# A one-layer hybrid decoder trunk: stick-breaking scans that read PSUM, full-width low products, one engine for four copies, and the second gate's row built in another stage

## The chip, the cores and the metric

One core of a Trainium2 chip runs the kernel. The metric is the device time of one execution in microseconds (us), as the median of several runs. Five engines work side by side, each through its own instructions in a fixed order: TensorE (PE, matrix products and transposes), VectorE (DVE), ScalarE (ACT), GpSimd (POOL) and SyncE (SP), which issues most of the DMAs here. They wait for one another through semaphores.

## The reference

One layer, 1024 tokens, width 1024, float32. What is computed:

```python
mod = silu(c) @ ada_w + ada_b
sh1, sc1, g1, sh2, sc2, g2 = split(mod, 6)
h = rms_norm(x, norm1_g) * (1 + sc1) + sh1
x = x + g1 * (concat(GLA(h), Retention(h), StickBreaking(h)) @ w_out)
h = rms_norm(x, norm2_g) * (1 + sc2) + sh2
x = x + g2 * swiglu(h, ffn_wg, ffn_wu, ffn_wd)
out = rms_norm(x, final_g)
```

GLA is gated linear attention (4 heads, key width 32), Retention has 4 heads of width 64, and stick-breaking attention has 8 heads of width 64:

```python
z = q @ k.T / 8
attn[t, s] = sigmoid(z[t, s]) * prod(1 - sigmoid(z[t, j]) for s < j < t)    # s < t
```

## The kernel before

The program has stages. A prologue normalises the tokens and makes the first projections (to about 98 us of the profiled execution). Then comes the **mixer**, about 100 to 700 us: the rest of the input projection, the three mixers, and the output projection in two halves. The **up stage**, about 700 to 1155 us, makes the two SwiGLU products, and the **down stage** the last product and the output. A float32 product is made of three single-pass matmuls: each operand is split into a high part and a low part (`split`, `split_to`), and `mm3` (L68 to L70) multiplies high by high, low by high and high by low.

In the mixer the dense projections are a generator that yields after every few microseconds of matmuls. At each yield the streams `ada`, `gla`, `ret` and `sb` are advanced to where a hand-written pace puts them (`Stream`, L786 to L789). What comes out is then ordered by the tile scheduler, which lays the instructions of each engine in its own order; so a change in one place moves instructions in others.

**Stick-breaking** (`sb_stream`). For each of 8 heads and 8 blocks of 128 queries, `weights` makes scores `z` in PSUM, in groups of up to 512 columns: 96 groups in all, through two PSUM banks (pool `pz`, two buffers). ACT turns each `z` into two sigmoids in SBUF: `u` = sigmoid(-z) (L410) and `At` = sigmoid(z) (L411). A DVE scan from right to left turns `u` into a running product in place (L418), and POOL multiplies `At` by it (L58, tile `s_a`). PE transposes the weights (L435, one bank, `tr`), ACT and DVE split them into `s_th` and `s_tl`, and `products` multiplies them with the values, whose high and low halves stand side by side as 64 and 64 columns of one stationary tile `V` (L454 to L457, one bank, `av`). The high weights meet both halves. The low weights meet the high half only, so that those matmuls write 64 of the 128 partitions. ACT and DVE then add the two halves into `s_o` (L461, L462).

**Gated linear attention** (`gla_stream`). Four blocks of 256 tokens, seven levels each. At each level four strips of `q` are copied into a block tile `g_qb`, two by DVE and two by ACT (L607), PE multiplies (L612), and DVE masks and scales.

**Modulation rows.** `ada_vec` (L281) makes one 1024-wide slice of `mod`: DVE clears `grow`, and for each of eight 512 KB loads of `ada_w` ACT scales the tile by silu(c) and POOL adds it into `grow`. `ada_row` (L291) sums over partitions with two PE products with a tile of ones. `ada_stream` runs slices 3, 4, 5 and 2 in the mixer. Slice 5 is the second gate g2: it goes to DRAM (`d_g2`, L310) and is loaded again ahead of the down stage (L1077). Slice 2, the first gate, is folded into the weights of the output projection.

**Up stage.** For each of 11 column groups and two weights, seven products of 512 columns run through eight PSUM banks in rotation (`bank`, `nps`). POOL and DVE make sums of the weights (`operands`, tile `st`); at its start, `t1` to `t4` are sums and differences of the normalised tokens (tiles `x`, `hb`, `to`).

Of the kernel before, what the change touches and what calls it, by code (L numbers as in the profile page):

```python
# [7 lines left out]
F32 = mybir.dt.float32  # L8
# [3 lines left out]
ALU = mybir.AluOpType  # L12
# [27 lines left out]
def tile_hybrid(ctx, tc, x, c, ada_w, ada_b, norm1_g, norm2_g, w_in, gla_wa2, gla_ba,  # L40
# [235 lines left out]


    grow = const.tile([P, D], F32, name="grow")
    d_g2 = dram.tile([P, D], F32, name="d_g2")

    def ada_vec(i):  # L281
        DVE.memset(grow, 0.0)
        nc.scalar.dma_start(grow[0:1, :], ada_b[:, i * 1024:(i + 1) * 1024])
        for k in range(8):
            raw = gp.tile([P, 1024], F32, name="a_raw", bufs=2)
            nc.sync.dma_start(raw, aw[k * P:(k + 1) * P, i * 1024:(i + 1) * 1024])
            ACT.activation(raw, raw, AF.Copy, scale=sil[:, k:k + 1])  # L287
            tt(POOL, grow, grow, raw, ALU.add)
            yield

    def ada_row(i):  # L291
        yield from ada_vec(i)
        for b in range(2):
            ps = dn.tile([P, NH], F32, name="dn")
            PE.matmul(ps, ones, grow[:, b * NH:(b + 1) * NH], start=True, stop=True)
            ACT.copy(grow[:, b * NH:(b + 1) * NH], ps)
        yield
# [7 lines left out]
    def ada_stream():  # L305
        yield from ada_cols(3, B2)
        yield from ada_cols(4, modc[:, 0:8])
        DVE.scalar_tensor_tensor(out=A2, in0=modc[:, 0:8], scalar=1.0, in1=cols[:, 16:24], op0=ALU.add, op1=ALU.mult)
        yield from ada_row(5)
        nc.scalar.dma_start(d_g2, grow)  # L310
        yield from ada_row(2)


# [58 lines left out]
    def sb_stream(pool, pz, ptr, pav):  # L372
# [22 lines left out]
        def weights(ops_, i):  # L395
            Q, K1, K2, _ = ops_
            W = (i + 1) * P
            At = pool.tile([P, NH * (1 + i // 4)], F32, name=f"s_a{i // 4}", bufs=4)
            carry = None
            for c0 in ((512, 0) if W > 512 else (0,)):  # L400
                w = min(W - c0, 512)
                z = pz.tile([P, NH], F32, name="z")
                q = Q[:, i * P:(i + 1) * P]
                diag = c0 + w == W
                PE.matmul(z[:, :w], q, K1[:, c0:c0 + w], start=True, stop=False)
                PE.matmul(z[:, :w], q, K2[:, c0:c0 + w], start=False, stop=not diag)
                if diag:
                    PE.matmul(z[:, w - P:w], identb, maskb, start=False, stop=True)
                u = pool.tile([P, 520], F32, name="s_u", bufs=2)
                ACT.activation(u[:, :w], z[:, :w], AF.Sigmoid, scale=-0.125)  # L410
                ACT.activation(At[:, c0:c0 + w], z[:, :w], AF.Sigmoid, scale=0.125)  # L411
                if carry is None:
                    POOL.memset(u[:, w:w + 1], 1.0)
                else:
                    DVE.tensor_copy(u[:, w:w + 1], carry)
                carry = u[:, 0:1]
                ur = u[:, 0:w][:, ::-1]
                DVE.tensor_tensor_scan(ur, ur, zero.broadcast_to([P, w]), u[:, w:w + 1], op0=ALU.mult, op1=ALU.add)  # L418
                tt(POOL, At[:, c0:c0 + w], At[:, c0:c0 + w], u[:, 1:w + 1], ALU.mult)
            return At  # L420

# [25 lines left out]
        def products(hd, i, g, V, th, tl):  # L447
            if g == i // 2:
                acc_ps[0] = pav.tile([P, 256], F32, name="av")
            ps = acc_ps[0]  # L450
            for sj in (1, 0):
                s_ = 2 * g + sj
                if s_ == i:
                    PE.matmul(ps, V[:, s_, :, :], th[:, sj, :], start=True, stop=False)  # L454
                PE.matmul(ps[0:64], V[:, s_, 0, :], tl[:, sj, :], start=False, stop=False)
                if s_ != i:
                    PE.matmul(ps, V[:, s_, :, :], th[:, sj, :], start=False, stop=(s_ == 0))  # L457
            if g == 0:
                done_sb[0] += 1
                o2 = pool.tile([64, 256], F32, name="s_o2", bufs=2)  # L460
                ACT.copy(o2, ps[64:128])  # L461
                tt(DVE, o2, o2, ps[0:64], ALU.add)  # L462
                nc.sync.dma_start(d_mix[4 + hd // 2][i // 4][64 * (hd % 2):64 * (hd % 2) + 64, (i % 4 - 1) * P:(i % 4 + 1) * P], o2)
# [78 lines left out]
    def gla_stream(pool, pg):  # L542
# [33 lines left out]
        for bi in range(4):  # L576
# [23 lines left out]
            for l in range(NLEV):  # L600
                m = 1 << l
                nb = P // m
                kv = k32.rearrange("p (b e m) -> p b e m", e=2, m=m)
                qv = q32.rearrange("p (b e m) -> p b e m", e=2, m=m)
                for h in range(4):
                    r = slice(32 * h, 32 * h + 32)
                    (ACT.copy if h % 2 else DVE.tensor_copy)(  # L607
                        QB[l % 2][r, h, :].rearrange("p (b m) -> p b m", m=m), qv[r, :, 1, :])
                yield
                ps = pg.tile([P, 8, 64], F32, name="g")  # L610
                for c_ in range(2):
                    PE.matmul(ps[:, 4 * c_:4 * c_ + 4, :], k32[:, c_ * P:(c_ + 1) * P],  # L612
                              QB[l % 2][:, :, c_ * 64:(c_ + 1) * 64], start=(c_ == 0), stop=(c_ == 1))
                so = Sm.rearrange("p h (b e m) -> p h b e m", e=2, m=m)[:, :, :, 1, :]
                mk = gm[:, l * 64:(l + 1) * 64].rearrange("p (b m) -> p b m", m=m).unsqueeze(1).broadcast_to([P, 8, 64 // m, m])
                DVE.copy_predicated(so, mk, ps.rearrange("p h (b m) -> p h b m", m=m))
                Tv = T.rearrange("p (b e) -> p b e", e=2)
                tt(DVE, qv[:, :, 1, :], qv[:, :, 1, :], Tv[:, :, 0:1].broadcast_to([P, nb, m]), ALU.mult)
                tt(DVE, kv[:, :, 0, :], kv[:, :, 0, :], Tv[:, :, 1:2].broadcast_to([P, nb, m]), ALU.mult)
                if l == 2 and fin:  # L620
                    fin()
                    fin = None
                T2 = pool.tile([P, P], F32, name="g_t", bufs=2)[:, :nb]
                tt(DVE, T2, Tv[:, :, 0], Tv[:, :, 1], ALU.mult)
                T = T2
# [160 lines left out]
    gla = Stream(gla_stream(gp, pgp), [65, 0], [225, 76])  # L786
    ret = Stream(ret_stream(pgp), [216, 0], [248, 41])
    sb = Stream(sb_stream(sbp, pz, ptr, pav), [0, 0], [123.5, 60], [265, 152])
    ada = Stream(ada_stream(), [20, 0], [185, 36])  # L789
    active = [ada, sb]  # L790

    def in_units():
# [230 lines left out]
    for j in range(4):  # L1023
# [6 lines left out]
        for lst, r in ((t3, r12), (t2, r22), (t4, r21)):  # L1030
            op = halves(tp.tile([P, D], F32R, name="to"))
            lst.append(split_to((op[:, 0], op[:, 1]), r))

    for i in range(NF // 2):
        gate = None
        for w in range(2):
            c0, c1, c2, c3 = early[w] if i == 0 else first_two(i, w)
            silu(w, c0)
            mid = ("s2", t2), ("s3", t3), ("a22", t4), ("s1", t1)
            if i == w == 0:  # L1040
                p6, p7, p4, p5 = products(i, w, *mid)
            else:
                p6, p7, p4, p5 = None, None, None, None
            p6 = p6 if p6 is not None else products(i, w, mid[0])
            tt(DVE, c1, c1, p6, ALU.add)
            p7 = p7 if p7 is not None else products(i, w, mid[1])
            tt(DVE, c2, c1, p7, ALU.add)
            p4 = p4 if p4 is not None else products(i, w, mid[2])
            tt(DVE, c3, c2, p4, ALU.add)
            silu(w, c3)  # L1050
            p5 = p5 if p5 is not None else products(i, w, mid[3])
            tt(DVE, c2, c2, p5, ALU.add)
            tt(DVE, c1, c1, p5, ALU.add)
            silu(w, c2)
            tt(DVE, c1, c1, products(i, w, ("s4", b22)), ALU.add)
            silu(w, c1)
            if w == 0:
                gate = c0, c1, c3, c2
            else:


                a11, a21, a12, a22 = gate
                s3, s1, s4, s2 = c0, c1, c3, c2
                for g_, u_ in zip((a11, a21, a22, a12), (s3, s1, s2, s4)):
                    tt(POOL, g_, g_, u_, ALU.mult)
                tt(POOL, s3, a11, a21, ALU.subtract)
                tt(POOL, s2, a22, s3, ALU.subtract)
                tt(DVE, s1, a21, a22, ALU.add)
                tt(DVE, s4, a12, s2, ALU.subtract)
                for n, a in (("a11", a11), ("a12", a12), ("a22", a22), ("s3", s3), ("s2", s2), ("s1", s1), ("s4", s4)):  # L1070
                    nc.scalar.dma_start(d_g[i][n], a)
# [2 lines left out]

    nc.sync.dma_start(grow, d_g2)  # L1077
    xe.close()
    kp = ctx.enter_context(tc.tile_pool(name="kp", bufs=8))
    ct = [halves(kp.tile([P, D], F32, name="ct")) for t in range(8)]  # L1080
# [202 lines left out]
```

## Time and profile before

| | us |
|---|---|
| median of 3 runs | 1379.72 (1377.66 to 1384.37) |
| the profiled execution, its own time | 1378.98 |
| its span, first to last instruction | 1377.1 |
| PE busy | 1271.5 (92%) |
| DVE busy | 994.4 (72%) |
| POOL busy | 750.1 (54%) |
| ACT busy | 626.3 (45%) |

The span lies 1.9 us under the time of the same execution, and that time 0.7 us under the median. Busy shares are averages over stages with different limits: PE is busy nearly all the time in the up stage and has gaps in the mixer, so the mixer's waits are read by themselves. The granted clock of PE is at its upper level nearly everywhere and at the lower one in short pieces.

### The profile page before, as it was taken

The page shows a single profiled execution, that of the slowest core. Times are in us where ns is not written, and L with a number is a line of the kernel's source. Part 1 is how long each engine was busy: PE and PEld are TensorE (multiplying, and loading weights), DVE is VectorE, ACT ScalarE, POOL GpSimd, SP SyncE. Part 2 cuts the span into 40 slices and gives each one's busy share as a digit, 9 for nine tenths or more (in the row PEclk, how much of TensorE's full clock was granted, in tenths as well). Part 3 has the DMA queues.
Part 4 walks back from the last instruction along what each step waited for, and adds up shares of the span by engine and source line. Part 5 has one row for each costly group of instructions (what it writes and reads, how often), then busy time and mean ns, then how long its engine had stood idle before and what let it go on. Part 6 is the DMA issues. An engine that isn't in the chain of part 4 may idle for free.

```text
span 1377.1 us, 20202 instructions
## 1 busy us (share of the span) xinstructions
PE 1271.5 (92%) x7076; PEld 1096.4 (80%) x7076; DVE 994.4 (72%) x1376; ACT 626.3 (45%) x1198; POOL 750.1 (54%) x732
## 2 busy tenths in 40 slices
PE   2899998989979998998998999999999999999996
PEld 1678897779868888898986888888888887888874
DVE  5604666898798968888579756655666558989996
ACT  3445675565555645444365333323333324544344
POOL 4737445355473435674157555555455534647893
PEclk9999999999999999999998999999999999999998
DMA  9537536263443237413432333332332346755333
GB/s 308 186 101 224 161 108 196 89 177 104 136 141 89 62 101 237 148 50 101 150 121 86 107 115 114 101 110 89 107 107 93 107 143 221 246 165 187 116 122 123
DMA packets 141026, 187.62 MB, mean 136 GB/s; under 512 B 19230, under 2 KB 94167, under 8 KB 140923
## 3 DMA queue, kind: packets, MB, share of 16 engines
q1 hardware_dynamic: 112416, 148.90, 35.5%
q10 hardware_dynamic: 28508, 37.43, 7.9%
q8 instruction: 56, 0.92, 0.3%
q14 instruction: 46, 0.38, 0.1%
HBM read 138.77 MB, written 47.51 MB: 135 GB/s over the span
## 4 chain that ended last, share of the span: by engine, by line
PE 54%; DVE 22%; DMA 9%; issue 7%; POOL 4%; ACT 4%; SPq 0%; DVEq 0%; ACTq 0%; POOLq 0%
PE m L69 7%; PE m L70 7%; PE m L68 7%; PE dn L69 6%; PE dn L68 6%; PE dn L70 6%; DVE s_u L418 4%; PE tr L69 3%; PE tr L70 3%; PE tr L68 3%; DVE acc L210 3%; DMA a_raw<-in_ada_w_dram 2%; DVE to L58 2%; POOL grow L58 1%; DVE hl L58 1%
## 5 line engine op out<-in xcount | busy, mean ns | idle before, releaser
L68 PE MATMUL dn<-whi,hh 128*128 128x256 f32 (+1 forms) x768 | 224.0, 292 | 0.4 <-ACT st L337 0.3
L70 PE MATMUL dn<-whi,hl 128*128 128x256 f32 (+1 forms) x768 | 222.7, 290 | 0.0
L69 PE MATMUL dn<-wlo,hh 128*128 128x256 f32 (+1 forms) x768 | 221.4, 288 | 0.2 <-DVE wlo L58 0.2
L58 POOL TENSOR_TENSOR s_a<-s_a,s_u 128x128 f32<-128x128 f32 (+3 forms) x96 | 98.8, 1033 | 130.2 <-DVE s_u L418 66.5
L68 PEld LDWEIGHTS dn<-whi,hh 128*128 128x128 f32 x768 | 148.3, 193 | 2.8 <-ACT st L337 0.6
L69 PEld LDWEIGHTS dn<-wlo,hh 128*128 128x128 f32 x768 | 148.3, 193 | 1.8 <-DVE wlo L58 0.4
L70 PEld LDWEIGHTS dn<-whi,hl 128*128 128x128 f32 x768 | 148.2, 193 | 0.8
L418 DVE TENSOR_TENSOR_SCAN s_u<-s_u,zero 128x128 f32<-128x128 f32 (+3 forms) x96 | 119.1, 1248 | 33.2 <-ACT s_u L410 20.3
L58 POOL TENSOR_TENSOR st<-raw 128x512 f32<-128x512 f32 x44 | 68.8, 1563 | 89.0 <-DMA raw<-in_ffn_wg_dram 65.3
L58 POOL TENSOR_TENSOR grow<-grow,a_raw 128x1024 f32<-128x1024 f32 x32 | 79.5, 2484 | 47.0 <-ACT a_raw L287 25.3
L58 POOL TENSOR_TENSOR x<-x,x 128x512 f32<-128x512 f32 x55 | 78.7, 1432 | 41.5 <-DVE x L58 39.6
L64 ACT CAST s_th<-tr 128x512 fp32r<-128x512 f32 (+2 forms) x112 | 48.7, 435 | 63.0 <-DVE s_tl L58 36.2
L58 DVE TENSOR_TENSOR s_tl<-tr,s_th 128x512 fp32r<-128x512 f32 (+2 forms) x112 | 54.9, 490 | 30.0 <-ACT s_th L64 29.7
L58 DVE TENSOR_TENSOR x<-x,m 128x512 f32<-128x512 f32 x79 | 52.8, 682 | 22.1 <-PE m L70 21.1
L58 DVE TENSOR_TENSOR wlo<-raw,whi 128x1024 fp32r<-128x1024 f32 (+2 forms) x32 | 42.1, 1319 | 33.5 <-ACT whi L64 33.3
L58 DVE TENSOR_TENSOR wlo<-st,wlo 128x512 fp32r<-128x512 f32 x44 | 47.9, 1088 | 24.0 <-ACT wlo L914 23.3
L58 DVE TENSOR_TENSOR to<-whi,to 128x512 fp32r<-128x512 f32 x53 | 55.8, 1054 | 11.7 <-ACT to L914 11.7
L58 POOL TENSOR_TENSOR st<-raw,st 128x512 f32<-128x512 f32 x22 | 28.9, 1315 | 63.9 <-DVE whi L58 37.8
L914 ACT CAST to<-whi 128x512 fp32r<-128x512 f32 x53 | 32.9, 620 | 62.7 <-PE m L70 24.6
L914 ACT CAST wlo<-raw 128x512 fp32r<-128x512 f32 x33 | 20.5, 621 | 85.9 <-POOL x L58 64.6
L914 ACT CAST wlo<-st 128x512 fp32r<-128x512 f32 x44 | 27.4, 622 | 70.7 <-DVE x L58 29.4
L410 ACT ACTIVATE s_u<-z 128x128 f32<-128x128 f32 (+3 forms) x96 | 46.5, 491 | 28.0 <-POOL s_a L58 12.5
(374 smaller groups left out, 4079.8 us busy)
## 6 DMA issues: line engine op xcount, KB each, us to landing
a_raw<-in_ada_w_dram SPq DMA_DIRECT2D x32, 512.0 KB, 4.9
raw<-in_ffn_wg_dram SPq DMA_DIRECT2D x22, 512.0 KB, 3.9
raw<-in_ffn_wu_dram SPq DMA_DIRECT2D x22, 512.0 KB, 3.9
hb<-in_ffn_wd_dram SPq DMA_DIRECT2D x44, 256.0 KB, 3.6
d_g_s<-x ACTq DMA_DIRECT2D x44, 256.0 KB, 2.0
whi<-d_g_s SPq DMA_DIRECT2D x44, 256.0 KB, 3.1
raw<-in_w_in_dram SPq DMA_DIRECT2D x20, 512.0 KB, 3.9
d_g_a<-x ACTq DMA_DIRECT2D x33, 256.0 KB, 2.9
```

What stands on the lines that cost most here:

```text
L58: eng.tensor_tensor(out=o, in0=a, in1=b, op=op)
L64: ACT.copy(hi, src)
L68: PE.matmul(o, sh, mh, start=start, stop=False)
L69: PE.matmul(o, sh, ml, start=False, stop=False)
L70: PE.matmul(o, sl, mh, start=False, stop=stop)
L210: DVE.scalar_tensor_tensor(out=acc[:, cs_[s]], in0=ab[s, h][:, k, :], scalar=sil[:, 4 * h + k:4 * h + k + 1], in1=acc[:, cs_[s]], op0=ALU. ...
L410: ACT.activation(u[:, :w], z[:, :w], AF.Sigmoid, scale=-0.125)
L418: DVE.tensor_tensor_scan(ur, ur, zero.broadcast_to([P, w]), u[:, w:w + 1], op0=ALU.mult, op1=ALU.add)
L914: ACT.copy(op[0], src)
```

## The change

Four edits. The second sigmoid is written back into the PSUM bank of `z`, and the scan reads it there and writes `u` in SBUF; the sigmoid for `At` comes first. The low weights multiply both value halves. All four copies of a GLA level are on ACT. The row for g2 is made in the loop of the up stage, from its second column group on, through the buffers `hb`, and its two sums take banks of the up stage's rotation; the trip through DRAM is gone. The pace of `ada` ends at step 27 in place of 36.

```diff
-    d_g2 = dram.tile([P, D], F32, name="d_g2")
-
-    def ada_vec(i):
+    def ada_vec(i, raw_of=None):
         DVE.memset(grow, 0.0)
         nc.scalar.dma_start(grow[0:1, :], ada_b[:, i * 1024:(i + 1) * 1024])
         for k in range(8):
-            raw = gp.tile([P, 1024], F32, name="a_raw", bufs=2)
+            raw = raw_of() if raw_of else gp.tile([P, 1024], F32, name="a_raw", bufs=2)
             nc.sync.dma_start(raw, aw[k * P:(k + 1) * P, i * 1024:(i + 1) * 1024])
...
-    def ada_row(i):
-        yield from ada_vec(i)
+    def ada_row(i, raw_of=None, bank_of=None):
+        yield from ada_vec(i, raw_of)
         for b in range(2):
-            ps = dn.tile([P, NH], F32, name="dn")
+            ps = bank_of() if bank_of else dn.tile([P, NH], F32, name="dn")
...
-        yield from ada_row(5)
-        nc.scalar.dma_start(d_g2, grow)
         yield from ada_row(2)
...
                 u = pool.tile([P, 520], F32, name="s_u", bufs=2)
-                ACT.activation(u[:, :w], z[:, :w], AF.Sigmoid, scale=-0.125)
                 ACT.activation(At[:, c0:c0 + w], z[:, :w], AF.Sigmoid, scale=0.125)
+                ACT.activation(z[:, :w], z[:, :w], AF.Sigmoid, scale=-0.125)
...
-                DVE.tensor_tensor_scan(ur, ur, zero.broadcast_to([P, w]), u[:, w:w + 1], op0=ALU.mult, op1=ALU.add)
+                DVE.tensor_tensor_scan(ur, z[:, 0:w][:, ::-1], zero.broadcast_to([P, w]), u[:, w:w + 1], op0=ALU.mult, op1=ALU.add)
...
-                PE.matmul(ps[0:64], V[:, s_, 0, :], tl[:, sj, :], start=False, stop=False)
+                PE.matmul(ps, V[:, s_, :, :], tl[:, sj, :], start=False, stop=False)
...
                 for h in range(4):
                     r = slice(32 * h, 32 * h + 32)
-                    (ACT.copy if h % 2 else DVE.tensor_copy)(
-                        QB[l % 2][r, h, :].rearrange("p (b m) -> p b m", m=m), qv[r, :, 1, :])
+                    ACT.copy(QB[l % 2][r, h, :].rearrange("p (b m) -> p b m", m=m), qv[r, :, 1, :])
...
-    ada = Stream(ada_stream(), [20, 0], [185, 36])
+    ada = Stream(ada_stream(), [20, 0], [185, 27])
...
+    def next_bank():
+        nps[0] += 1
+        return bank(nps[0] - 1)
+
+    g2 = ada_row(5, lambda: tp.tile([P, D], F32, name="hb", bufs=4), next_bank)
     for i in range(NF // 2):
         gate = None
+        if i:
+            next(g2, None)
...
-    nc.sync.dma_start(grow, d_g2)
+    for _ in g2:
+        pass
     xe.close()
```

The scheduler's order moves with it. On DVE, in one level of gated linear attention (`g_s` is the masked product, `g_k` and `g_q` the scaled strips, `s_tl` and `s_u` belong to stick-breaking), it was:

```order
L616 COPY_PREDICATED g_s<-gm,g 128x256x2
L58 TENSOR_TENSOR g_k<-g_k,g_t 128x64x2
L607 COPY g_qb_2484<-g_q 32x128 x2
L58 TENSOR_TENSOR g_t<-g_t 128x32
L58 TENSOR_TENSOR g_q<-g_q,g_t 128x16x8
```

and is now:

```order
L612 COPY_PREDICATED g_s<-gm,g 128x128x4
L58 TENSOR_TENSOR g_k<-g_k,g_t 128x32x4
L58 TENSOR_TENSOR g_t<-g_t 128x16
L58 TENSOR_TENSOR g_q<-g_q,g_t 128x8x16
L58 TENSOR_TENSOR s_tl<-tr,s_th 128x512
```

The pair of copies is out of DVE's order in every level. On ACT, at the start of the fifth head of stick-breaking, the sigmoids of two groups and what surrounds them were:

```order
L410 ACTIVATE s_u<-z 128x128
L411 ACTIVATE s_a_3713<-z 128x128
L296 COPY grow<-dn 128x512
L410 ACTIVATE s_u<-z 128x256
L411 ACTIVATE s_a_3762<-z 128x256
```

and are now:

```order
L407 ACTIVATE s_a_3688<-z 128x128
L408 ACTIVATE z<-z 128x128
L407 ACTIVATE s_a_3731<-z 128x256
L408 ACTIVATE z<-z 128x256
L64 CAST s_th<-tr 128x512
```

The sigmoid that the scan needs stands second, and it writes `z`. On POOL, at the start of the up stage (`hb<-x,hb`, `x<-x,hb` and `hb<-hb,x` make the token sums, `st` the weight sums), it was:

```order
L58 TENSOR_TENSOR x_8282<-x_8282,x_8353 128x512
L58 TENSOR_TENSOR hb<-hb,x_8248 128x512
L58 TENSOR_TENSOR hb<-hb 128x512
L58 TENSOR_TENSOR x_8265<-x_8265,hb 128x512
L58 TENSOR_TENSOR hb<-hb 128x512
L58 TENSOR_TENSOR hb<-hb,x_8265 128x512
L58 TENSOR_TENSOR hb<-hb 128x512
L58 TENSOR_TENSOR st<-raw 128x512
L58 TENSOR_TENSOR st<-st,raw 128x512
```

and is now:

```order
L58 TENSOR_TENSOR hb<-hb,x_8206 128x512
L58 TENSOR_TENSOR x_8223<-x_8223,hb 128x512
L58 TENSOR_TENSOR grow<-grow,hb 128x1024
L58 TENSOR_TENSOR hb<-hb,x_8223 128x512
L58 TENSOR_TENSOR grow<-grow,hb 128x1024 x2
L58 TENSOR_TENSOR st<-raw 128x512
L58 TENSOR_TENSOR grow<-grow,hb 128x1024
L58 TENSOR_TENSOR st<-st,raw 128x512
L58 TENSOR_TENSOR st<-raw 128x512
L58 TENSOR_TENSOR grow<-grow,hb 128x1024
```

Though the loop asks for one step of the row per column group, the scheduler draws all eight additions to the start of the stage, among the last token sums and the first weight sums. `hb<-hb` were differences of the down weights, loaded ahead; they stand later now.

## Rows read from the trace of the kernel before

**Rows 1.** Busy time by stretch: window, length, PE, PEld, DVE, ACT, POOL, PEclk, DMA, GB/s.

```profile
100.00:700.00 600.00, 552.69 (x3927) 508.20 (x3925) 457.82 (x719) 326.36 (x677) 302.52 (x397) 0.98 0.45 133
...
780.00:1150.00 370.00, 370.00 (x1634) 306.38 (x1633) 222.32 (x295) 119.98 (x202) 188.02 (x133) 1.00 0.36 114
```

**Rows 2.** Waits of PE, 100 to 700 us: total us, times, longest us.

```profile
PE av L454 <- DVE s_o L58: 14.1, 6, 4.3
PE tr L435 <- DVE s_tl L58: 11.2, 11, 2.5
PE g L612 <- DVE g_k L58: 4.8, 4, 2.4
...
PE z L405 <- ACT s_a L411: 1.9, 4, 0.6
```

**Rows 3.** Groups of DVE by shape, 100 to 700 us: busy us, mean ns, idle before.

```profile
L418 DVE TENSOR_TENSOR_SCAN s_u<-s_u,zero 128x512 f32<-128x512 f32 x48 | 76.7, 1599 | 7.4 <-ACT s_u L410 5.6
...
L58 DVE TENSOR_TENSOR s_tl<-tr,s_th 128x512 fp32r<-128x512 f32 x48 | 32.7, 680 | 20.5 <-ACT s_th L64 20.4
...
L607 DVE COPY g_qb<-g_q 32x128 f32<-32x128 f32 x56 | 19.7, 351 | 0.5
...
L58 DVE TENSOR_TENSOR wlo<-raw,wlo 128x512 fp32r<-128x512 f32 x1 | 0.7, 678 | 0.0
```

**Rows 4.** The scan's line: ns min/median/max of all shapes.

```profile
L418 DVE TENSOR_TENSOR_SCAN s_u<-s_u,zero x96: 468/1272/3120, 118.0 to 612.0; 128x512 f32<-128x512 f32 x48, 128x128 f32<-128x128 f32 x16, 128x256 f32<-128x256 f32 x16, 128x384 f32<-128x384 f32 x16
```

**Rows 5.** Timeline of DVE, 280 to 292.4 us: start, us, instruction.

```profile
280.72 2.98 DVE L418 TENSOR_TENSOR_SCAN s_u<-s_u,zero 128x512 f32<-128x512 f32 x1 [0.40 <-ACT s_u L410]
...
285.01 2.54 DVE L607 COPY g_qb<-g_q 32x128 f32<-32x128 f32 x2
...
288.71 1.28 DVE L418 TENSOR_TENSOR_SCAN s_u<-s_u,zero 128x512 f32<-128x512 f32 x1
```

**Rows 6.** Timeline of POOL, the same stretch.

```profile
280.21 2.41 POOL L58 TENSOR_TENSOR grow<-grow,a_raw 128x1024 f32<-128x1024 f32 x1 [3.36 <-ACT a_raw L287]
...
285.06 2.41 POOL L58 TENSOR_TENSOR grow<-grow,a_raw 128x1024 f32<-128x1024 f32 x1
```

**Rows 7.** Timeline of PE, the same stretch; in brackets the idle time before.

```profile
285.24 1.10 PE L612 MATMUL g<-g_qb,g_k 128*128 128x256 f32 x4 [1.99 <-ACT s_o L461]
...
292.19 0.55 PE L454 MATMUL av<-s_th,s_v 128*128 128x256 f32 x1 [3.10 <-DVE s_o L58]
```

**Rows 8.** Busy time by stretch, behind those gaps.

```profile
286.00:300.00 14.00, 10.90 (x62) 10.14 (x61) 12.56 (x22) 5.89 (x12) 5.78 (x4) 0.76 0.58 152
```

**Rows 9.** Groups of ACT by shape, 100 to 700 us.

```profile
L287 ACT ACTIVATE a_raw<-a_raw,sil 128x1024 f32<-128x1024 f32 x32 | 36.9, 1154 | 35.1 <-DMA a_raw<-in_ada_w_dram 33.5 <-POOL s_a L58 1.6
...
L607 ACT COPY g_qb<-g_q 32x128 f32<-32x128 f32 x56 | 16.7, 298 | 21.5 <-DVE g_q L58 6.6 <-PE g L612 4.7 <-POOL g_qb L571 3.2
```

**Rows 10.** Groups of POOL by shape, 100 to 700 us.

```profile
L58 POOL TENSOR_TENSOR grow<-grow,a_raw 128x1024 f32<-128x1024 f32 x32 | 79.5, 2484 | 47.0 <-ACT a_raw L287 25.3 <-DMA grow<-in_ada_b_dram 18.6 <-DVE s_tl L58 2.7
```

**Rows 11.** Timeline of PE, 300 to 325 us: the two kinds of value products.

```profile
307.42 0.28 PE L457 MATMUL av<-s_th,s_v 128*128 128x256 f32 x1
307.53 0.28 PE L455 MATMUL av<-s_tl,s_v 128*64 128x256 f32 x1
307.65 0.28 PE L457 MATMUL av<-s_th,s_v 128*128 128x256 f32 x1
```

**Rows 12.** Busy time by stretch at the start of the up stage.

```profile
720.00:740.00 20.00, 14.03 (x50) 9.82 (x50) 20.00 (x17) 14.48 (x24) 18.14 (x11) 0.83 0.20 62
740.00:760.00 20.00, 18.31 (x73) 14.76 (x74) 16.91 (x21) 6.34 (x11) 13.27 (x10) 0.91 0.35 110
760.00:780.00 20.00, 20.00 (x89) 16.54 (x89) 15.50 (x22) 6.61 (x12) 13.74 (x10) 1.00 0.36 116
```

**Rows 13.** A group of POOL, 710 to 790 us.

```profile
L58 POOL TENSOR_TENSOR hb<-hb 128x512 f32<-128x512 f32 x4 | 6.2, 1548 | 4.5 <-DMA hb<-in_ffn_wd_dram 4.5
```

**Rows 14.** A group of PE, 100 to 700 us.

```profile
L295 PE MATMUL dn<-grow,ones 128*128 128x512 f32 x8 | 4.3, 616 | 0.0
```

## The prediction

> **What bounds the kernel now.** I read first the busy time by stretch. In the up stage PE is busy 370.00 of 370.00 us at full clock: nothing that is taken from another engine there can shorten it. In the mixer, 100 to 700 us, PE is busy 552.69 of 600, so it stands idle 47.3 us, and a mean granted clock of 0.98 says that about 2% more, 12 us, is lost in pieces at the lower level [rows 1]. Those 59 us are what the first three edits can win. Second, the waits of PE in that stretch: the two longest sums end at DVE, at the add that empties the bank of the value products (14.1 us in 6 waits) and at the low split that frees the transpose bank (11.2 in 11), and the third at a DVE scaling (4.8 in 4). These are 30.1 of the 47.3 us [rows 2]. DVE itself is busy 457.82 of 600 us [rows 1]. So PE waits because DVE comes late to short jobs that PE needs, each behind other work in DVE's fixed order.
>
> Third, what that other work is. A 512-column scan takes 1599 ns in the mean [rows 3], yet 1.28 us at 288.71 us [rows 5]; the longest scan of all takes 3120 [rows 4]. The long ones run beside a POOL operation: the scan of 2.98 us that starts at 280.72 lies over a 2.41 us addition of POOL that starts at 280.21, and the pair of copies that takes 2.54 us at 285.01 lies over the next one at 285.06 [rows 5, 6]. The low split `s_tl`, which reads one operand in PSUM, has a mean of 680 ns over 48, the same as the 678 of an undisturbed split that reads two from SBUF [rows 3]. So with one operand in PSUM the stretching is gone, and there is no surcharge for reading PSUM.
>
> Fourth, one piece of the timeline shows how that reaches PE: it stood idle 1.99 us before 285.24 and 3.10 us before 292.19 [rows 7]. The first gap lies behind the stretched scan, the second behind the stretched copies, with DVE working nearly without a break in between. [...]
>
> **The change part by part.** *Scans.* With the stretching gone, 48 x (1.60 - 1.28) = 15.3 us leave DVE. Of the 48 shorter scans I count nothing in the sum.
> [...]
>
> *Copies.* 56 copies, 19.7 us, leave DVE [rows 3]. ACT does their like in 298 ns, 16.7 us for 56, and takes them on [rows 9]. ACT is busy 326.36 of 600 us [rows 1], and the g2 row takes 8 x 1.154 = 9.2 us away from it there [rows 9], so it ends about 7 us fuller: room enough. A level's four strips now follow one another, 4 x 0.30 instead of 2 x 0.30 us, on 28 levels; I cost that at nothing, since PE has dense products to do in the meantime. If that cover failed it would be at most 28 x 0.6 = 16.8 us.
>
> *The g2 row.* Eight POOL additions of 2484 ns, 19.9 us [rows 10], leave the mixer, a quarter of the 32 that stretch two-operand work on DVE. What DVE's other instructions gain from that I leave out.
>
> Together DVE loses 15.3 + 19.7 = 35 us of 458. How much of that is PE's? In the piece shown, the scan shrinks by 2.98 - 1.28 = 1.70 of the gap of 1.99, and the pair of copies goes entirely, 2.54 of the gap of 3.10 [rows 5, 7]: 4.2 of 5.1 us, 83%. A gap whose run of DVE work holds neither piece gives 0. Between those ends I take the middle, 40%: 12.0 of the 30.1 us of waits, and 40% of the 12 us lost to the clock, 4.8, since the low pieces stand behind such gaps. **Gain 16.8 us**, with 0 and 35 as its ends (83% of 42.1).
>
> *The bank of `z`.* It is given back when the scan has ended, and no longer when ACT has read it. PE waits today for ACT at 4 of 96 groups, 1.9 us in all [rows 2]. Each such wait grows by the scan, 1.28 to 1.60 us: 4 x 1.28 = 5.1 us if DVE starts at once. Behind a wait for `z` on PE stand dense products, which wait too. Against it, the scheduler knows the new wait and may leave more work between two groups. Ends 0 and, as the rival below, 31; I take 2, nearest to the few waits that exist.
>
> *Low products.* 160 matmuls now fill 128 columns. In the row of products, the 64-column one starts at 307.53 and the next at 307.65, 0.12 us; the 128-column one at 307.42 is followed after 0.11 [rows 11]. So the moving 256 columns set the pace, and the edit costs nothing on PE. Were every one to pay the difference of these slots in the other direction, 160 x 0.01 = 1.6 us, it would be a gain; I take 0.
>
> *The row in the up stage.* Two products of 616 ns go into a stage where PE never rests: 1.2 us [rows 1, 14]. The eight additions, 19.9 us, are drawn to the start of the stage, where four differences of the down weights, 6.2 us, had been [rows 13]: 13.7 us more of POOL. From 720 to 780 us POOL is busy 18.14 + 13.27 + 13.74 = 45.2 of 60, so they fit into the 14.8 us that are free, but only just; PE is idle 6.0 us of the first 20 there, and DVE is busy all of them [rows 12]. Most token sums stand ahead of the additions in POOL's order, and the first weight sums between them. Cost between 0 and 13.7; I take 2, near the low end, since PE is full from 760 on. Eight loads of 512 KB and 9.2 us of ACT lie under the stage's DMA share of 0.36 and ACT's 120 of 370 us [rows 1].
>
> Sum: -16.8 + 2 + 1.2 + 2 = **-11.6 us**. The profiled execution took 1378.98, so 1367.4; it lies 0.7 us under the median of the runs, so against that I say **1368 us**.
>
> **The rivals.** *More than forecast.* If the other gaps are like the piece shown, 83% of 42.1 us come back: 35 - 5 = 30 us, 1350. For it: the three DVE jobs of rows 2 are short, and 35 us go from the queue ahead of them. Against: many gaps stand behind masks, splits and rotations that stay.
>
> *Nothing arrives.* DVE gets lighter, but PE waits for the next engine: ACT, with 7 us more, stands just ahead of DVE in every split, and the sigmoid that the scan needs now comes second. Or the scan from PSUM stretches all the same, as it still reads the zero operand in SBUF. Then costs and gain cancel: 1376 to 1384.
>
> *Slower: the two banks of `z` become the pace.* A bank is now held through both sigmoids, DVE's queue and the scan. Today PE waits at 4 of 96 groups [rows 2]. If a quarter of the groups, 24, came to wait for a scan of 1.28 us, that would be 31 us, and with the gain of 16.8 and the 3.2 of the up stage the time would be 1397. It decides at about 13 groups, where the waits eat the gain. For it: there are only two banks, and long scans of up to 3.1 us exist now [rows 4]. Against: the scans that hold them are to become short.
> [...]
>
> **How the numbers follow.** The forecast has 0.50, its own range 1358 to 1375; more than forecast 0.13; nothing arrives 0.25; slower through `z` 0.12. The range of 8 in 10 reaches from 1350 to 1386: below it half of the first rival, above it most of the last one. About 0.5%, 6.9 us, is what a measurement of this kernel can tell from no change, so no change means 1372.8 to 1386.6. Faster: 0.44 of the forecast and 0.13, 0.57. Same: 0.06 of the forecast, 0.23 of "nothing arrives", 0.29 in all. Slower: 0.12 and 0.02, 0.14.
>
> **What would show it.** Right: scans of 512 columns with a mean near 1.28 us and no long ones; DVE in the mixer near 420 us; the sums of PE's waits for `s_o` and `s_tl` down by about 12 us, and the second output half starting about 15 us earlier; at 720 to 780 us PE idle 2 us more than now. Wrong: PE waits for `z` ended by DVE scans of more than 10 us; the mean scan still above 1.4; or the start of the up stage losing more than 6 us, with PE behind POOL's additions.

## The result and the profile after

| | before | after |
|---|---|---|
| median (lowest to highest), us | 1379.43 (1377.66 to 1384.37) | 1357.41 (1355.40 to 1359.89) |
| span of the profiled execution, us | 1377.1 | 1353.6 |
| ratio to before, 95% interval | | 0.9847 [0.9828, 0.9866] |

The change makes the kernel 22 us faster; 1368 was forecast, with a range of 1350 to 1386. The likeliest case's own range, 1358 to 1375, was missed by 0.6 us.

**Where the time came from.** The first up-stage product of a token tile `hh` marks the end of the mixer, and the last one nearly the end of the up stage. The view by tile `m` gives first and last start, of before:

```profile
L68 PE MATMUL m<-hh,whi x88: 389/389/776, 703.1 to 1140.4; 128*128 128x512 f32 x88
```

and of after:

```profile
L68 PE MATMUL m<-hh,whi x88: 389/389/793, 673.9 to 1117.8; 128*128 128x512 f32 x88
```

The mixer ends 29.2 us earlier. The up stage, from the first to the last of these starts, grew by 6.6, from 437.3 to 443.9, and what follows fell by 0.9. Together that is -23.5, the difference of the spans. The two sides of the change are thus of opposite sign, and each is larger than forecast.

Busy time by stretch (columns as in [rows 1]), the mixer to its end and the first 100 us of the up stage, before:

```profile
100.00:703.10 603.10, 555.79 (x3952) 511.30 (x3951) 460.65 (x725) 328.57 (x681) 302.52 (x397) 0.98 0.45 133
703.10:803.10 100.00, 91.54 (x403) 73.62 (x402) 78.60 (x93) 46.38 (x79) 67.62 (x51) 0.95 0.33 110
```

and after:

```profile
100.00:673.90 573.90, 544.59 (x3947) 506.32 (x3946) 410.57 (x669) 334.77 (x727) 272.38 (x388) 0.99 0.44 131
673.90:773.90 100.00, 87.67 (x382) 68.04 (x381) 88.84 (x84) 52.15 (x83) 83.70 (x53) 0.97 0.44 142
```

In the mixer PE's idle time (length less busy time) falls from 47.3 to 29.3 us, by 18.0, and its busy time by 11.2. Of these 11.2, 2.3 are the g2 row's sums, which left the mixer: 4.3 us in [rows 14], and 2.0 in after:

```profile
L294 PE MATMUL dn<-grow,ones 128*128 128x512 f32 x4 | 2.0, 590 | 0.0
```

The clock accounts for about 5, by estimate: the trace has 27.3 us of the mixer at the lower level before and 17.1 in after, and at that level the granted clock is 0.50 (before, 292 to 298 us), so half of such time counts as lost. The rest was not explained. DVE loses 50 us. At the start of the up stage it is the other way round: PE's idle time goes from 8.5 to 12.3 us, while DVE gains 10.2 us and POOL 16.1. Over the whole up stage, before and after:

```profile
703.10:1140.40 437.30, 428.84 (x1891) 352.90 (x1890) 276.40 (x354) 151.26 (x255) 237.90 (x170) 0.99 0.34 111
```

```profile
673.90:1117.80 443.90, 431.57 (x1896) 352.17 (x1895) 291.90 (x354) 159.94 (x265) 259.54 (x178) 0.99 0.37 119
```

The 6.6 us are 3.9 of idle time, all of it in the first 100 us, and 2.7 of busy time.

PE's waits in the mixer of after (100 to 673.9 us), against [rows 2]:

```profile
PE z L402 <- DVE s_u L415: 6.4, 5, 2.4
PE tr L432 <- DVE s_tl L58: 5.2, 6, 2.3
...
PE av L451 <- DVE s_o L58: 2.4, 3, 1.7
...
PE g L628 <- DVE g_k L58: 0.8, 1, 0.8
```

The waits for `s_o` and `s_tl`, 25.3 us before, are 7.6 now, and the one for `g_k` is 0.8, at another product, in place of 4.8, so that of 30.1 us 8.4 are left. In return PE waits for the scan to give back `z`, 6.4 us at 5 groups, where it waited 1.9 for ACT: -21.7 + 4.5 = -17.2 of the 18.0.

DVE's groups by shape (100 to 700 us) and the scan's line (min/median/max), against [rows 3, 4]:

```profile
L415 DVE TENSOR_TENSOR_SCAN s_u<-z,s_u,zero 128x512 f32<-128x512 f32 x48 | 61.3, 1277 | 9.6 <-ACT z L408 4.3 <-POOL s_u L410 2.3 <-PE av L454 1.7
...
L415 DVE TENSOR_TENSOR_SCAN s_u<-z,s_u,zero x96: 470/1138/1284, 117.6 to 592.8; 128x512 f32<-128x512 f32 x48, 128x128 f32<-128x128 f32 x16, 128x256 f32<-128x256 f32 x16, 128x384 f32<-128x384 f32 x16
```

No scan is stretched any more: the longest takes 1.284 us where it was 3.120. The mean of 512 columns, 1277 ns, is that of an undisturbed scan from SBUF (1.28 us, [rows 5]).

### The profile page after: what moved, and what is told of

Same layout as the page of the kernel before. It is cut to its first block, busy times and chain, and to the rows that moved or that the text cites. A ratio compares the mean times of both kernels' runs of the same rounds, so it can differ in the third digit from the quotient of the medians.

```text
span 1353.6 us, 20070 instructions
## 1 busy us (share of the span) xinstructions
PE 1263.5 (93%) x7076; PEld 1091.0 (81%) x7076; DVE 960.0 (71%) x1320; ACT 640.6 (47%) x1254; POOL 740.4 (55%) x732
## 4 chain that ended last, share of the span: by engine, by line
PE 66%; DVE 15%; DMA 6%; issue 5%; ACT 4%; POOL 4%; SPq 1%; ACTq 0%; DVEq 0%; POOLq 0%
PE dn L69 9%; PE dn L68 9%; PE dn L70 9%; PE m L69 6%; PE m L70 6%; PE m L68 6%; PE tr L69 3%; PE tr L70 3%; PE tr L68 3%; DVE to L58 3%; DVE acc L210 2%; DVE hl L58 2%; PE tr L432 2%; DVE ct L58 1%; DMA raw<-in_w_out_dram 1%
## 5 line engine op out<-in xcount | busy, mean ns | idle before, releaser
L415 DVE TENSOR_TENSOR_SCAN s_u<-z,s_u,zero 128x128 f32<-128x128 f32 (+3 forms) x96 | 96.5, 1009 | 33.0 <-ACT z L408 20.4
L58 POOL TENSOR_TENSOR grow<-grow,a_raw 128x1024 f32<-128x1024 f32 x24 | 59.5, 2478 | 32.2 <-ACT a_raw L286 19.4
L64 ACT CAST s_th<-tr 128x512 fp32r<-128x512 f32 (+2 forms) x112 | 48.7, 435 | 54.1 <-PE tr L432 29.6
L58 DVE TENSOR_TENSOR wlo<-st,wlo 128x512 fp32r<-128x512 f32 x44 | 48.6, 1106 | 25.9 <-ACT wlo L910 25.3
L910 ACT CAST wlo<-st 128x512 fp32r<-128x512 f32 x44 | 27.3, 621 | 65.7 <-DVE x L58 26.1
L407 ACT ACTIVATE s_a<-z 128x128 f32<-128x128 f32 (+3 forms) x96 | 47.2, 492 | 23.3 <-PE z L405 15.4
```

What stands on the lines that cost most here:

```text
L58: eng.tensor_tensor(out=o, in0=a, in1=b, op=op)
L64: ACT.copy(hi, src)
L415: DVE.tensor_tensor_scan(ur, z[:, 0:w][:, ::-1], zero.broadcast_to([P, w]), u[:, w:w + 1], op0=ALU.mult, op1=ALU.add)
L910: ACT.copy(op[0], src)
```

## The experiments

### Each edit undone, and each alone

First, each edit was undone in the changed kernel by putting its old lines back (the hunks are those of the diff above; one line or a few of each here). The scheduler lays another order in every kernel of this section, so a number holds for an edit together with the order that it brings.

```diff
-                DVE.tensor_tensor_scan(ur, z[:, 0:w][:, ::-1], zero.broadcast_to([P, w]), u[:, w:w + 1], op0=ALU.mult, op1=ALU.add)
+                DVE.tensor_tensor_scan(ur, ur, zero.broadcast_to([P, w]), u[:, w:w + 1], op0=ALU.mult, op1=ALU.add)
```

> The changed kernel with the scans back on SBUF (both sigmoids into SBUF, the scan's first). Queue theory (PE waits because DVE's queue is long; relief of DVE is what counts): the 23 us of stretched scans come back to DVE, PE's waits for the bank of the value products and for the transpose bank rise by 8 to 12 us, time 1366 to 1371. Row theory (the second gate's row, taken out of the mixer, gave most): 1357 to 1361. Order theory (the gain is an accident of the scheduler's new order): no forecast from DVE's time; any value, with DVE's waits not moving along.

```diff
-                    ACT.copy(QB[l % 2][r, h, :].rearrange("p (b m) -> p b m", m=m), qv[r, :, 1, :])
+                    (ACT.copy if h % 2 else DVE.tensor_copy)(
+                        QB[l % 2][r, h, :].rearrange("p (b m) -> p b m", m=m), qv[r, :, 1, :])
```

> The changed kernel with two of the four copies of a level back on DVE. Queue theory: 19.7 us or, with less POOL work beside them, about 15 us come back to DVE, time 1363 to 1368. Row theory: 1357 to 1361. A rival of its own: four copies in a row on ACT lengthen each level, so undoing them gains, 1350 to 1356.

```diff
-                PE.matmul(ps, V[:, s_, :, :], tl[:, sj, :], start=False, stop=False)
+                PE.matmul(ps[0:64], V[:, s_, 0, :], tl[:, sj, :], start=False, stop=False)
```

> The changed kernel with the low weights on the high half of the values alone. Queue theory: the moving columns set PE's pace, so 1356 to 1359, no change. Order theory: the scheduler lays another order, and the time moves by over 4 us either way.

```diff
+        yield from ada_row(5)
+        nc.scalar.dma_start(d_g2, grow)
         yield from ada_row(2)
...
-        if i:
-            next(g2, None)
```

> The changed kernel with the second gate's row back in the mixer (and the old pace of that stream). Queue theory: 20 us of POOL additions come back, which stretch what DVE still reads from SBUF twice; the mixer loses 3 to 6 us and the start of the up stage gains 3 to 4, so 1356 to 1360. Row theory: 1369 or more.

Then each was made alone in the kernel before, by the same hunks the other way round.

```diff
-                DVE.tensor_tensor_scan(ur, ur, zero.broadcast_to([P, w]), u[:, w:w + 1], op0=ALU.mult, op1=ALU.add)
+                DVE.tensor_tensor_scan(ur, z[:, 0:w][:, ::-1], zero.broadcast_to([P, w]), u[:, w:w + 1], op0=ALU.mult, op1=ALU.add)
```

> The kernel before with the scans reading PSUM and nothing else. Queue theory: 23 us of stretching leave DVE, time 1366 to 1371, mean 512-column scan near 1.28 us. If the two banks of z are what costs: PE's waits for z, ended by scans, of over 10 us, and 1378 or more.

```diff
-                    (ACT.copy if h % 2 else DVE.tensor_copy)(
-                        QB[l % 2][r, h, :].rearrange("p (b m) -> p b m", m=m), qv[r, :, 1, :])
+                    ACT.copy(QB[l % 2][r, h, :].rearrange("p (b m) -> p b m", m=m), qv[r, :, 1, :])
```

> The kernel before with all four copies of a level on ACT and nothing else. Queue theory: 19.7 us leave DVE, 1369 to 1374. If the longer level counts on ACT: 1380 or more.

```diff
-                PE.matmul(ps[0:64], V[:, s_, 0, :], tl[:, sj, :], start=False, stop=False)
+                PE.matmul(ps, V[:, s_, :, :], tl[:, sj, :], start=False, stop=False)
```

> The kernel before with full-width low products and nothing else. Queue theory: 1378 to 1381. Order theory: moved by over 4 us either way.

```diff
-        yield from ada_row(5)
-        nc.scalar.dma_start(d_g2, grow)
...
+        if i:
+            next(g2, None)
```

> The kernel before with the second gate's row in the up stage and nothing else. Queue theory: a quarter of POOL's additions leave the mixer and with them a quarter of the stretching, 8 to 10 us of DVE; mixer 4 to 7 us shorter, start of the up stage 3 to 4 longer: 1375 to 1379. Row theory: 1367 or less.

| edit | alone: us | ratio to before | undone: us | over after's 1357.41 |
|---|---|---|---|---|
| scan | 1359.29 | 0.9872 [0.9842, 0.9901] | 1375.77 | +18.4 |
| copies | 1380.66 | 1.0019 [1.0000, 1.0038] | 1360.75 | +3.3 |
| low products | 1377.75 | 1.0013 [0.9990, 1.0036] | 1357.27 | -0.1 |
| g2 row | 1376.45 | 0.9996 [0.9983, 1.0010] | 1358.30 | +0.9 |

The scan edit carries nearly the whole gain in time, alone and in company. The low products are worth nothing that these runs can tell. The copies are worth nothing alone, and about 3 us beside the others, where the two ranges (1359.32 to 1363.22, and after's) just overlap. The queue theory of the expectations, by which a microsecond of DVE is worth the same wherever it is saved, missed at both: the scans lie 4.8 us (undone) and 6.7 us (alone) beyond its ranges, the copies 2.3 and 6.7 us short of them.

With the scans undone, PE's waits of [rows 2] come back (100 to 695.3 us):

```profile
PE tr L432 <- DVE s_tl L58: 10.6, 12, 2.9
PE g L608 <- DVE g_k L58: 4.8, 3, 2.2
...
PE av L451 <- DVE s_o L58: 3.6, 3, 2.0
...
PE g L628 <- DVE g_k L58: 1.3, 1, 1.3
```

They are 20.3 us, 11.9 more than the 8.4 of after.

The g2 row changes the time by nothing that can be told, but by two effects that cancel, as the view by tile `m` of the row alone shows:

```profile
L68 PE MATMUL m<-hh,whi x88: 389/389/793, 695.3 to 1139.1; 128*128 128x512 f32 x88
```

The mixer ends 7.8 us earlier than before, and the up stage takes 443.8 us for 437.3. Both are more than expected (4 to 7, and 3 to 4). Beside the other edits the same shows, with the row undone:

```profile
L68 PE MATMUL m<-hh,whi x88: 387/389/775, 686.4 to 1123.1; 128*128 128x512 f32 x88
```

Against after the mixer ends 12.5 us later and the up stage is 7.2 us shorter, though this execution, of 1361.42 us, was the longest of its four.

### Why the scan edit gains: DVE's time or the buffers?

The edit does two things: it shortens the scans, and it lets ACT write both sigmoids without waiting for a free `u`. The first test keeps the short scan and adds DVE time in front of it:

```diff
+                DVE.memset(u[:, 0:w // 2], 0.0)
                 DVE.tensor_tensor_scan(ur, z[:, 0:w][:, ::-1], zero.broadcast_to([P, w]), u[:, w:w + 1], op0=ALU.mult, op1=ALU.add)
```

> The kernel before with the scans alone reading PSUM, and ahead of each scan a DVE clear of half as many columns of its own output (which the scan then overwrites): about 0.2 us each, 20 us in all, about what the stretching had cost, but spread evenly and never long. Queue theory (DVE's mean load is what counts): the gain of the scans alone, 19 us, goes for the most part, 1370 to 1378. Long-holds theory (what hurts are the few scans and other operations of 2 to 3 us that PE's short jobs stand behind, not DVE's mean load): 1360 to 1365. Buffer theory (ACT no longer waits for the buffer u, and scores and scans have four buffers in place of two): 1358 to 1363.

It took 1379.26 us, 1.0004 [0.9985, 1.0024]: the whole gain is gone. DVE's groups by shape (100 to 700 us):

```profile
L419 DVE TENSOR_TENSOR_SCAN s_u<-z,s_u,zero 128x512 f32<-128x512 f32 x48 | 61.0, 1272 | 4.8 <-ACT z L411 3.4
...
L418 DVE MEMSET s_u<- 128x256 f32 x48 | 13.1, 272 | 13.2 <-POOL s_a L58 8.1 <-POOL s_u L413 3.4 <-DMA g_gg<-d_gg 1.2
```

and its mixer beside that of the scan edit alone, which ends at 685.0; first the scan edit alone, then with the padding:

```profile
100.00:685.00 585.00, 549.70 (x3947) 506.12 (x3946) 431.05 (x725) 328.39 (x681) 287.74 (x396) 0.98 0.46 137
```

```profile
100.00:703.80 603.80, 555.88 (x3924) 510.40 (x3923) 452.41 (x814) 325.89 (x679) 282.67 (x396) 0.97 0.44 132
```

The scans are as short as with the edit alone, yet 21.4 us more of DVE, at the scans' place, cost 18.8 us of the mixer. Of the three theories only the queue's comes near, and its range is missed by 1.3 us; the other two said 1365 at most. One thing blurs it: the clearing must wait for a free `u`, and behind its 13.2 us of idle time stands mostly POOL, which still reads `u`. That is no idle time on top: DVE stands idle 154.0 us in the mixer of the edit alone and 151.4 with the padding, since the scans then wait less for ACT's `z`. Whether the wait's earlier place in DVE's order costs something was not tried. Nor does the loss return in the waits that the change had cut, first with the scan edit alone, then with the padding:

```profile
PE tr L435 <- DVE s_tl L58: 8.1, 6, 2.0
PE g L612 <- DVE g_k L58: 5.7, 5, 3.2
```

```profile
PE g L613 <- DVE g_k L58: 5.4, 4, 2.4
...
PE av L455 <- DVE s_o L58: 3.3, 3, 2.4
PE tr L436 <- DVE s_tl L58: 3.2, 5, 1.2
```

With the smaller ones (0.6 for `s_o` alone, 1.1 for a second `g_k` padded) that is 14.4 and 13.0 us, while PE's idle time goes from 35.3 to 47.9. The padding thus shows that DVE's time at this place is worth the gain, and not that it comes back by the same jobs.

The second test keeps the edit and gives back the old wait of ACT for `u`, by one column written there ahead of the second sigmoid:

```diff
+                ACT.copy(u[:, w + 1:w + 2], zero)
                 ACT.activation(z[:, :w], z[:, :w], AF.Sigmoid, scale=-0.125)
```

> The kernel before with the scans alone reading PSUM, and ahead of the second sigmoid an ACT copy of one column into the scan's output buffer, so that ACT waits for that buffer as it did before; it adds some 16 us of short copies to ACT. Buffer theory: 1370 to 1378, and ACT waits for POOL again, over 10 us. Queue and long-holds theories: ACT has room, 1358 to 1364.

It took 1361.14 us, 0.9870 [0.9839, 0.9901], and its mixer ended at 686.8. ACT did wait for POOL again, 37.7 us where it was 12.5 before, and the gain stayed (waits of ACT, first of before, 100 to 700 us, then of this run, 100 to 686.8 us):

```profile
ACT s_u L410 <- POOL s_a L58: 12.5, 10, 3.3
```

```profile
ACT s_u L411 <- POOL s_a L58: 37.7, 37, 4.0
```

So the buffers are not the reason. What is left of the edit is the time that the scans lost.

### Why the copies gain nothing

The kernel before, without DVE's two copies per level. Nobody makes them, so half of the strips' products in gated linear attention are left out of the output; ACT's load stays as it was.

```diff
-                    (ACT.copy if h % 2 else DVE.tensor_copy)(
-                        QB[l % 2][r, h, :].rearrange("p (b m) -> p b m", m=m), qv[r, :, 1, :])
+                    if h % 2:
+                        ACT.copy(QB[l % 2][r, h, :].rearrange("p (b m) -> p b m", m=m), qv[r, :, 1, :])
```

> The kernel before without DVE's two strip copies per level of gated linear attention; nobody makes them, so half of the strips' products are left out of the output. ACT's load is that of the kernel before. Copies alone, moved to ACT, gave 1380.7 us, no gain, although 20 us left DVE. If DVE's time at that place counts and ACT's four copies in a row ate the gain: 20 us off DVE at the scans' rate (15 to 20 us of DVE, 19 us of time) gives 1358 to 1370. If DVE's time at that place is not on PE's path, because what waits behind it is held by something else: 1373 to 1381, like the copies moved to ACT. In both cases DVE busy in the mixer falls by about 20 us.

It took 1369.78 us, 0.9954 [0.9939, 0.9969] to the 1377.14 of before in the same series. Its mixer by stretch:

```profile
100.00:695.30 595.30, 554.37 (x3948) 510.55 (x3947) 440.55 (x669) 328.45 (x681) 303.30 (x397) 0.98 0.45 134
```

and that of the copies moved to ACT:

```profile
100.00:706.00 606.00, 560.45 (x3948) 515.96 (x3946) 437.37 (x669) 344.21 (x737) 312.10 (x397) 0.96 0.45 132
```

The number lies just inside the first theory's bounds, by the ratio (6.3 us, 4.3 to 8.4) between the two theories, and both hold in part. DVE's 20.1 us are worth 7.8 us of the mixer here, PE's idle time falling from 47.3 to 40.9; that is 0.39 us for each of DVE's (by one profile each), where the scan edit alone had 18.1 us of the mixer for 29.6 (0.61) and the padding 18.8 for 21.4 (0.88). And moved to ACT, with 15.6 us more there than before, the copies lose it all: PE is idle 45.5 us, and busy 6.1 us longer than without them at a clock of 0.96. One line of PE's waits with the copies on ACT shows a part of it (1.9 in 4 before, [rows 2]):

```profile
PE z L405 <- ACT s_a L411: 4.8, 4, 2.7
```

How the rest splits between ACT's lateness and the clock was not tried.

### The g2 row held back

The start of the up stage is crowded, and nothing needs the row there. In this version of the changed kernel the row's `grow` is cleared from a result `c0` of the second column group, times zero, so that the additions can't be drawn ahead of it.

```diff
+    def clear_late():
+        for b in range(2):
+            DVE.tensor_scalar(grow[:, b * NH:(b + 1) * NH], late[0], 0.0, None, op0=ALU.mult)
...
-        if i:
-            next(g2, None)
...
                 s3, s1, s4, s2 = c0, c1, c3, c2
+                if i:
+                    late.append(c0)
+                    next(g2, None)
```

> The changed kernel with the second gate's row held back: its start value is cleared from a tile that the up stage makes in its second column group, so that POOL's eight additions come behind the token sums. If those additions are what the start of the up stage lost (4 to 5 us between the 2592nd and the 3000th dense product): 1352 to 1356. If the loss comes from elsewhere (the down weights' differences that moved, the loads): 1356 to 1359.

It took **1351.27 us** (1348.49 to 1354.10), 0.9798 [0.9760, 0.9837]: the best of all, with no overlap with after's range, and 0.7 us below what was expected. The additions by tile `grow` (min/median/max, first and last start) in after:

```profile
L58 POOL TENSOR_TENSOR grow<-grow,hb x8: 2413/2728/2920, 714.5 to 757.2; 128x1024 f32<-128x1024 f32 x8
```

and held back, with the stretches of its mixer and of the first 100 us of its up stage:

```profile
L58 POOL TENSOR_TENSOR grow<-grow,hb x8: 2392/2684/2865, 767.0 to 804.7; 128x1024 f32<-128x1024 f32 x8
```

```profile
100.00:673.80 573.80, 545.81 (x3942) 507.43 (x3941) 410.07 (x668) 334.64 (x727) 271.72 (x388) 0.98 0.44 130
673.80:773.80 100.00, 92.13 (x408) 74.42 (x407) 79.56 (x92) 49.58 (x82) 64.10 (x47) 0.95 0.34 111
```

The mixer is unchanged. In the start of the up stage PE's idle time is 7.9 us, where after has 12.3 and before had 8.5, and DVE is back from 88.8 to 79.6 us. What DVE lost there shows in two groups of DVE by shape, after (673.9 to 773.9 us):

```profile
L58 DVE TENSOR_TENSOR whi<-st,whi 128x512 fp32r<-128x512 f32 x8 | 12.4, 1554 | 0.1
...
L58 DVE TENSOR_TENSOR x<-x,m 128x512 f32<-128x512 f32 x11 | 7.3, 678 | 0.2
```

and held back (673.8 to 773.8 us):

```profile
L58 DVE TENSOR_TENSOR x<-x,m 128x512 f32<-128x512 f32 x15 | 9.9, 677 | 0.0
...
L58 DVE TENSOR_TENSOR whi<-st,whi 128x512 fp32r<-128x512 f32 x9 | 8.1, 905 | 0.1
```

The split with both operands in SBUF takes 1554 ns beside POOL's additions and 905 without them; the add with one operand in PSUM takes 678 and 677. The same holds for the token sums' split, 1497 ns in after and 1223 held back:

```profile
L58 DVE TENSOR_TENSOR to<-x,to 128x512 fp32r<-128x512 f32 x8 | 11.9, 1497 | 0.0
```

```profile
L58 DVE TENSOR_TENSOR to<-x,to 128x512 fp32r<-128x512 f32 x8 | 9.7, 1223 | 0.0
```

PE waits for these splits. Its longest waits in the same 100 us of after:

```profile
PE dn L69 <- DVE to L58: 5.5, 5, 2.6
...
PE m L70 <- DVE whi L58: 1.1, 2, 0.7
```

Held back, the first is 3.7 us and the second is gone. All of PE's waits together are 4.4 us fewer, 3.7 of them at splits of DVE, 0.7 at one of ACT. So the row in the up stage costs mostly by the effect that the scan edit removes from the mixer. Most of the row's loads and of ACT's scalings moved with the additions (the DMA share falls from 0.44 to 0.34) and were not tried apart, but no wait of PE ends at a DMA there.

## Why the prediction was right, and where its sizes were off

- **What bounds the kernel: right.** DVE's late short jobs held PE. The waits for `s_o`, `s_tl` and `g_k` fell by 21.7 us, and rose by 11.9 with the scans undone; the padded scan gave the time back, though in other waits. [Rows 7] names ACT's `s_o` at the end of the first gap, where the prediction put it down to the scan. The timeline of before fits the prediction:

```profile
284.41 0.68 DVE L58 TENSOR_TENSOR g_k<-g_k,g_t 128x128 f32<-128x128 f32 x1
284.86 0.37 ACT L461 COPY s_o<-av 64x256 f32<-64x256 f32 x1
...
285.20 0.73 PEld L612 LDWEIGHTS g<-g_qb,g_k 128*128 128x128 f32 x4 [2.16 <-ACT s_v L424]
```

PE's weight load began at 285.20, before `s_o` had ended (285.23) and 0.11 us after `g_k`, which the product reads and which stood behind the scan.
- **Scans that read PSUM are not stretched: right.** 48 scans lost 15.4 us (15.3 forecast). The shorter ones, counted as nothing, lost another 7.5: 20.1, 12.7 and 10.2 us by shape before, 16.1, 11.8 and 7.6 after. The mean of 512 columns was 1599 ns with all inputs in SBUF and 1277 with `z` in PSUM, and the longest scan of any shape 3120 and 1284. Side by side at the start of the up stage of after, the group with two operands in SBUF took 1554 ns and the one with one 678.
- **The gain term: mis-sized.** "Between those ends I take the middle, 40%" gave 12.0 us of PE's waits and 4.8 of the clock. Measured were 21.7 of the 30.1 us, 72%, and about 5 from the clock, so that the waits alone were mis-sized. The middle was a choice without a row; the only piece looked at said 83%, and it was nearer. The clock's part was taken for what stands behind DVE's gaps. Of the six low pieces in the mixer of before, four do: behind [rows 7]'s second gap the clock was 0.50 (292 to 298 us), behind waits of 4.26 us for `s_o`, 1.30 and 1.05 for `s_tl` it was 0.66 (216 to 221), 0.62 (264 to 268.5) and 0.58 (657 to 661). One stands behind ACT (0.57 at 602 to 606), and one behind no gap at all (0.52 at 186 to 193, with PE busy all of 170 to 186). With the cost for `z` taken off the forecast for the mixer was -14.8 us, the measurement -29.2. It is also made up otherwise: alone, the scans shorten the mixer by 18.1 us, the row, "left out", by 7.8, and the copies, more than half of the 35 us of DVE that the sum counted, lengthen it by 2.9.
- **The bank of `z`: right in kind.** 2 us were taken and 4.5 came: PE's waits for `z` ended by `s_a` and `s_u` went from 1.9 to 6.4 us, at 5 groups. The slower rival needed 13.
- **Copies: wrong in one step.** "ACT ... ends about 7 us fuller: room enough" and the cover "costed at nothing" both failed. Alone the copies on ACT gain nothing, and dropping them gains 6.3 us. It went unseen in the sum, as the copies' 19.7 us of DVE were put on one footing with the scans' 15.3.
- **Low products: right**, at nothing that the runs can tell.
- **The row in the up stage: mis-sized.** 1.2 + 2 us were forecast, 2.7 of busy time and 3.9 of idle time came, the latter inside the bounds of 0 and 13.7 that stood beside the 2. [Rows 14] shows eight instructions, 4.3 us, for two rows of `mod`, so one row costs PE four, about 2.2 us, and not two. "They fit into the 14.8 us that are free" looked at POOL's time alone; DVE was busy 10.2 us longer in the first 100 us, and 9.3 of these go when the additions are held back.

Sum of the steps: forecast -14.8 + 3.2 = -11.6; measured, by spans, -29.2 + 6.6 - 0.9 = -23.5. The rival "more than forecast" (1350) was the closer one for the mixer, and was missed through the up stage; with the row held back, the time is 1351. That the total came within 11 us of the forecast is in part luck: the mixer was off by 14.4 us, and the up stage, off by 3.4 the other way, hid some of it.

## What to carry to other kernels

Where DVE work with two operands in SBUF runs beside POOL work, look at the longest of each shape and not only at the mean (the longest scan took 3120 ns here, the mean of 512 columns 1599); an operand that already passes through PSUM can stay there (1284 and 1277). A microsecond taken from an engine is worth what stands behind it: here about 0.4 us at the copies and 0.6 at the scans, and nothing once ACT had to do the copies instead. A piece that a scheduler may draw ahead needs a true dependence to keep it out of a crowded place.

## What the runs showed of the hardware

- A scan of 512 columns took 1277 ns from PSUM, in the mean of 48 (after), and 1.28 us from SBUF with POOL idle beside it (before, at 288.71 us, [rows 5]).
- A sigmoid of 512 columns took ACT as long into PSUM as into SBUF, 601 and 600 ns. The two groups of after, 100 to 700 us:

```profile
L408 ACT ACTIVATE z<-z 128x512 f32<-128x512 f32 x48 | 28.8, 601 | 0.0
L407 ACT ACTIVATE s_a<-z 128x512 f32<-128x512 f32 x48 | 28.8, 600 | 7.2 <-PE z L405 6.4 <-PE z L403 0.5
```

- The granted clock of the mixer was 0.96 to 0.99 over these kernels, and went its own way: with the low products undone, PE's idle time in the mixer was as in after (29.7 us against 29.3), and its busy time 5.7 us longer at 0.97:

```profile
100.00:680.00 580.00, 550.30 (x3943) 511.46 (x3942) 412.19 (x669) 335.22 (x727) 269.92 (x388) 0.97 0.44 129
```

That profiled execution took 1363.56 us, the longest of its four, whose median is 1357.27. So a few microseconds of busy time in one profile are not yet an effect of the edit.
